# Differential attention inside a two-layer block: score products on 64 rows, alternating between the two maps

## The chip, the cores and the metric

The kernel runs on one core of a Trainium2 chip. A core has a matrix engine, TensorE (PE in the profile, with its weight loads shown as PEld), a vector engine (DVE), a scalar engine (ACT), a general engine (POOL), and a queue (SP) that here issues all transfers between the chip's memory and the on-chip memory, and within the latter. Products are accumulated in a small memory of their own, PSUM. The metric is the time of one launch in microseconds, as the median of several runs.

## What is computed

The reference is two layers of a block over 512 latent tokens x and 256 context tokens ctx, with width 1024. Layer 0 mixes tokens with differential attention, layer 1 with a short gated convolution; each is followed by a SwiGLU feed-forward part, with RMSNorm and adaLN modulation ahead of every part. The change lies in the attention of layer 0, cut here to what matters:

```python
def diff_attention(h, hc, wqkv, lam, subln_g, wo, cos, sin, layer_idx, need_ctx):
    ...
    scale = HEAD_DIM ** -0.5                      # HEAD_DIM = 64, DA_HEADS = 8
    def project(t):
        q, k, v = jnp.split(t @ wqkv, 3, axis=-1)
        return (q.reshape(B, n, DA_HEADS, 2, HEAD_DIM),
                k.reshape(B, n, DA_HEADS, 2, HEAD_DIM),
                v.reshape(B, n, DA_HEADS, DA_VDIM))
    def attend(qb, kk, vv):
        s = jnp.einsum('bqhmd,bkhmd->bhmqk', qb, kk).astype(jnp.float32) * scale
        p = jax.nn.softmax(s, axis=-1)
        p = p[:, :, 0] - lam_full * p[:, :, 1]
        return jnp.einsum('bhqk,bkhe->bqhe', p.astype(vv.dtype), vv)
    ...
```

Each head has two score maps (m = 0 and 1), each from 64 of the head's 128 query and key components. The softmax of the second map, times a learned factor, is taken from that of the first, and the difference is applied to the values. The 512 latent queries look at 768 keys, latent and context.

## The kernel before

Activations are held transposed, with features on the 128 partitions and tokens along the free dimension. All large products are made from a high and a low part of each float32 operand: `split` (lines 53 to 55) rounds the source to the high part on ACT and has DVE subtract it for the low part. `mm3` (line 77) then issues three products, high by high, high by low and low by high.

`finish_q` and `finish_k` take the projected queries and keys of a head out of PSUM, apply the rotation (`rope`, on ACT, DVE and POOL) and split them into `qt` and `kt`. Partitions 0 to 63 belong to map 0, 64 to 127 to map 1. `halves_to` (line 432) then moves them with eight transfers a head, all on the SP queue (line 438): for each map it puts the 64 rows of the queries twice on top of each other, for high and low (`qs`), and the keys' high part above their low part (`ks`). With 128 rows filled that way, one product adds two of the four partial products at once: query-high and query-low each meet the stack of key-high and key-low, so that four products of the parts come from two instructions.

`attend` (line 508) goes over the four query blocks of a head, 32 blocks of 128 queries in all. For each block and map it makes scores S of 128 x 768 in a PSUM tile (line 528): two key ranges (512 and 256 columns) by two products. The tag "S" has two buffers, so the tile of one map is free again when the exponential of the same place in the block before is done. Then come a row maximum on DVE (line 532), the exponential on ACT (line 536), the combination of the two maps on DVE (line 546), six transposes on PE (line 551), and for every second block the product with the values (`po`). Between the blocks stand generators that make the projections of later heads (`psq`, `psk`, `pskc`, `psv`), the adaLN rows (`ada`, `araw`) and, at the end, the output projection (`poa`, `pob`).

The order on each engine is not written out by hand: a scheduler with a timeline of its own places every instruction once its operands are due, so score products and projections are interleaved on PE. Within `attend` nothing is fixed before the change.

Of the kernel before, what the change touches and what calls it, by code (L numbers as in the profile page):

```python
# [11 lines left out]
F32 = mybir.dt.float32  # L12
F32R = mybir.dt.float32r
# [5 lines left out]
P = 128  # L19
# [5 lines left out]
def block_kernel(  # L25
# [11 lines left out]
    nc = tc.nc  # L37
    T = x.shape[1]
# [4 lines left out]
    KV = T + C  # L43
# [9 lines left out]
    def split(hi, lo, src):  # L53
        nc.scalar.copy(hi, src)  # L54
        nc.vector.tensor_tensor(lo, src, hi.bitcast(F32), op=ALU.subtract)  # L55
# [55 lines left out]
    psB = tc.alloc_tile_pool(name="psB", bufs=2, space=PSUM)  # L111
# [8 lines left out]

    for tag, n, bufs in (
        [(f"Or{h}", 512, 1) for h in range(NH)] + [("qs0", 1024, 2), ("qs1", 1024, 2)]
        + [("e", 768, 3), ("pth", 768, 3), ("ptl", 768, 3), ("ks0", 768, 2), ("ks1", 768, 2)]
        + [(f"v{p}{t}", 256, 2) for t in range(KB) for p in "hl"]
        + [("sq", 512, 1), ("dg0", 512, 1), ("dg1", 512, 1)]
        + [(t, 4, 2) for t in ("sv", "sr", "rh", "rl")] + [(t, 4, 3) for t in ("rr", "mx")] + [("ss", 8, 2), ("den", 8, 2)]
        + [("ld", 2, 1)]
        + [("araw", 1024, 2), ("ada", 1024, 1), ("qt", 1024, 1), ("kt", 1536, 1), ("rcos", 512, 1), ("rsin", 512, 1)]
        + [("sw", 512, 1), ("rt", 512, 2)]
    ):  # L130
        ap.tile([P, n], F32, tag=tag, bufs=bufs, name=f"place_{tag}")
# [4 lines left out]
    xt_dram = nc.dram_tensor("xt_spill", [DB, P, T], F32, kind="Internal").ap()  # L136

    rows = lambda v: v.rearrange("(j p) -> j p", p=P)
    st1, st2 = (ap.tile([P, P], F32, tag=t, name=n) for t, n in (("ks1", "st1"), ("ks1", "st2")))
    nc.vector.memset(st1, 0.0)  # L140
    nc.vector.memset(st2, 0.0)
    nc.sync.dma_start(st1[0:8, :], rows(c[0]))
# [26 lines left out]
    cn = [nat(ctx, t, "qs1", 2, f"cn{t}") for t in range(CB)]  # L169
# [37 lines left out]
    def nat_rstd(src, tag, name):  # L207

        nb = len(src)
        ss = ap.tile([P, 8], F32, tag="ss", name=f"ss{name}")  # L210
        for t in range(nb):
            for f in range(2):
                junk = ap.tile([P, 512], F32, tag="sq", bufs=1, name=f"junk{name}")
                nc.scalar.activation(
                    junk, src[t][:, f * 512:(f + 1) * 512], AF.Square,
                    accum_out=ss[:, t + 4 * f:t + 4 * f + 1],
                )
        v = ap.tile([P, 4], F32, tag="sv", name=f"sv{name}")[:, :nb]
        nc.vector.tensor_tensor(v, ss[:, :nb], ss[:, 4:4 + nb], op=ALU.add)
        nc.vector.tensor_scalar(v, v, 1.0 / D, EPS, op0=ALU.mult, op1=ALU.add)  # L220
        r = ap.tile([P, 4], F32, tag="sr", name=f"sr{name}")[:, :nb]
        nc.gpsimd.tensor_tensor(r, v, mhalf[:, :nb], op=ALU.pow)
        ps = spread(r, nb, "pt", name)
        o = ap.tile([P, 512], F32, tag=tag, bufs=2 if tag == "ks0" else 1, name=f"rs{name}")[:, :nb * P]
        nc.vector.tensor_copy(o, ps)
        return o

# [37 lines left out]

    XT0 = [ap.tile([P, T], F32, tag=f"Or{k}", bufs=1, name=f"XT{k}") for k in range(DB)]
    rx = nat_rstd(xn, "sw", "x")
    for k in range(0, DB, 2):
        pt = psB.tile([P, 2, T], F32, tag="S", name=f"ptx{k}")
        for a in range(2):  # L270
# [2 lines left out]
            nc.vector.tensor_copy(XT0[k + a], pt[:, a, :])  # L273
        if k == 0:
            ada0(0, raws0)
    rc = nat_rstd(cn, "ks0", "c")
    ctt = [ap.tile([P, 4, C], F32, tag="araw", name=f"ct{i}") for i in range(2)]
    CT = [ctt[k // 4][:, k % 4, :] for k in range(DB)]
    for i in range(2):
        pt = psB.tile([P, 4, C], F32, tag="S", name=f"ptc{i}")  # L280
        for a in range(4):
# [3 lines left out]
        for a in (0, 2):  # L285
            nc.scalar.copy(ctt[i][:, a:a + 2, :], pt[:, a:a + 2, :])
    vps = [psB.tile([P, 1024], F32, tag="S", name=f"vps{i}") for i in range(2)]
    qps = psB.tile([P, 512], F32, tag="acc", name="qps")
# [140 lines left out]
        eng.tensor_tensor(r, r, s, op=ALU.add)  # L429
        return r  # L430

    def halves_to(dst, src, both):

        for m in range(2):
            s = src[64 * m:64 * m + 64]
            for d in range(2):
                o = dst[m][64 * d:64 * d + 64]
                nc.sync.dma_start(
                    o.bitcast(F32), (s if both else s[:, d, :]).bitcast(F32)
                )  # L440

    def finish_q(h, ps):

        r = rope(ps, HD ** -0.5, f"q{h}")
        qt = ap.tile([P, 2, T], F32R, tag="qt", bufs=1, name=f"qt{h}")
        split(qt[:, 0, :], qt[:, 1, :], r)
        q = [ap.tile([P, 2, T], F32R, tag=f"qs{m}", name=f"qs{h}_{m}") for m in range(2)]
        halves_to(q, qt, True)
        return q

    def finish_k(h, ps, psc):

        r = rope(ps, None, f"k{h}")
        kt = ap.tile([P, 2, KV], F32R, tag="kt", bufs=1, name=f"kt{h}")
        split(kt[:, 0, T:], kt[:, 1, T:], psc)
        split(kt[:, 0, :T], kt[:, 1, :T], r)
        ks = [ap.tile([P, KV], F32R, tag=f"ks{m}", name=f"ks{h}_{m}") for m in range(2)]
        halves_to(ks, kt, False)
        return ks

    def finish_v(g, t, ps):
# [46 lines left out]
    def attend(h, between, after=None):  # L508
        q, ks, vs = Q[h], K[h], V[h // 2]
        vc = slice((h % 2) * P, (h % 2) * P + P)  # L510
        O = ap.tile([P, T], F32, tag=f"Or{h}", bufs=1, name=f"O{h}")
        den = ap.tile([P, 2, TB], F32, tag="den", name=f"den{h}")
        for pr in range(2):
            pts = []
            for kh in range(2):
                pts.append(
                    (ap.tile([P, 3, 256], F32R, tag="pth", bufs=3, name=f"pth{h}_{pr}_{kh}"),
                     ap.tile([P, 3, 256], F32R, tag="ptl", bufs=3, name=f"ptl{h}_{pr}_{kh}"))
                )
            for s in range(2):  # L520
                qb = 2 * pr + s
                e = []
                mx = ap.tile([P, 2], F32, tag="mx", bufs=3, name=f"mx{h}_{qb}")
                for m in range(2):
                    S = psB.tile([P, 1024], F32, tag="S", name=f"S{h}_{qb}_{m}")
                    for a, b in ((0, 512), (512, KV)):
                        for j in range(2):
                            nc.tensor.matmul(  # L528
                                S[:, a:b], q[m][:, j, qb * P:(qb + 1) * P], ks[m][:, a:b],
                                start=(j == 0), stop=(j == 1),  # L530
                            )
                    nc.vector.tensor_reduce(  # L532
                        out=mx[:, m:m + 1], in_=S[:, :KV], axis=AX.X, op=ALU.max, negate=True
                    )
                    em = ap.tile([P, KV], F32, tag="e", bufs=3, name=f"e{h}_{qb}_{m}")
                    nc.scalar.activation(  # L536
                        em, S[:, :KV], AF.Exp, bias=mx[:, m:m + 1], accum_out=den[:, m, qb:qb + 1]
                    )
                    e.append(em)

                rr = ap.tile([P, 1], F32, tag="rr", bufs=3, name=f"rr{h}_{qb}")
                nc.vector.reciprocal(rr, den[:, 1, qb:qb + 1])
                nc.vector.scalar_tensor_tensor(
                    rr, rr, nlam, den[:, 0, qb:qb + 1], op0=ALU.mult, op1=ALU.mult
                )
                nc.vector.scalar_tensor_tensor(e[0], e[1], rr, e[0], op0=ALU.mult, op1=ALU.add)
                for kh in range(2):
                    pt = psB.tile([P, 512], F32, tag="pt", name=f"pt{h}_{qb}_{kh}")[:, :3 * P]
                    for i in range(3):
                        k = 3 * kh + i  # L550
                        nc.tensor.transpose(pt[:, i * P:(i + 1) * P], e[0][:, k * P:(k + 1) * P], ident)
                    cs = slice(s * P, (s + 1) * P)
                    split(pts[kh][0][:, :, cs], pts[kh][1][:, :, cs], pt.rearrange("p (k c) -> p k c", c=P))
                between()
            po = psB.tile([P, 512], F32, tag="pt", name=f"po{h}_{pr}")[:, :256]
            for k in range(KB):
                ph, pl = pts[k // 3]
                mm3(po, vs[k][0][:, vc], vs[k][1][:, vc], ph[:, k % 3, :], pl[:, k % 3, :], k == 0, k == KB - 1)
            nc.scalar.copy(O[:, pr * 256:(pr + 1) * 256], po)
            if after:  # L560
                On[h] = O
                after(pr, den)
        On[h] = O
        if not after:
            later.append(subnorm(h, den, 0, TB))
# [395 lines left out]
```

## Time and profile before

| what | value |
|---|---|
| median of 3 runs | 1371.27 us (1370.04 to 1371.96) |
| the profiled execution, its own time | 1369.84 us |
| its span, first to last instruction | 1368.1 us |
| PE busy | 1312.1 us, 7052 products |
| DVE busy | 780.4 us |
| ACT busy | 529.6 us |
| POOL busy | 244.8 us |
| DMA, 16 engines | 44.7% of their time, 181.65 MB |

How to read it: the span is what the profile sees of the profiled execution, and the remaining 1.7 us lie around it. Products on PE are pipelined: a product's duration reaches from its start to its result, and the next one starts long before that, so the cost of one product in a stream is the distance between two starts. The heads run from about 108 us (first score product) to about 401 us (last).

### The profile page before, as it was taken

The page shows a single profiled execution, that of the slowest core. Times are in us where ns is not written, and L with a number is a line of the kernel's source. Part 1 is how long each engine was busy: PE and PEld are TensorE (multiplying, and loading weights), DVE is VectorE, ACT ScalarE, POOL GpSimd, SP SyncE. Part 2 cuts the span into 40 slices and gives each one's busy share as a digit, 9 for nine tenths or more (in the row PEclk, how much of TensorE's full clock was granted, in tenths as well). Part 3 has the DMA queues.
Part 4 walks back from the last instruction along what each step waited for, and adds up shares of the span by engine and source line. Part 5 has one row for each costly group of instructions (what it writes and reads, how often), then busy time and mean ns, then how long its engine had stood idle before and what let it go on. Part 6 is the DMA issues. An engine that isn't in the chain of part 4 may idle for free.

```text
span 1368.1 us, 18008 instructions
## 1 busy us (share of the span) xinstructions
PE 1312.1 (96%) x7052; PEld 1128.1 (82%) x7052; DVE 780.4 (57%) x1043; ACT 529.6 (39%) x872; POOL 244.8 (18%) x197
## 2 busy tenths in 40 slices
PE   6889899899999999999999999999999999999997
PEld 4678799798888988888888889888988888888887
DVE  6886976777886766776753255444473333332322
ACT  6655646454555432333222244222362232232222
POOL 3244635524314100000001041000340000000000
PEclk9999999999999999999999999999999999999999
DMA  8957633623432666666643333333333333333321
GB/s 291 271 151 219 189 101 124 152 80 93 135 97 80 197 206 200 219 222 203 212 128 96 100 93 93 93 98 88 92 93 99 102 92 93 106 91 109 94 78 62
DMA packets 238742, 182.79 MB, mean 134 GB/s; under 512 B 6937, under 2 KB 220226, under 8 KB 238658
## 3 DMA queue, kind: packets, MB, share of 16 engines
q1 hardware_dynamic: 238658, 181.65, 44.7%
q8 instruction: 55, 0.90, 0.3%
q14 instruction: 29, 0.24, 0.1%
HBM read 162.75 MB, written 4.19 MB: 122 GB/s over the span
## 4 chain that ended last, share of the span: by engine, by line
PE 79%; DVE 8%; DMA 4%; ACT 4%; issue 2%; POOL 2%; SPq 0%; DVEq 0%; ACTq 0%; POOLq 0%
PE po_fo L78 6%; PE po_fo L79 6%; PE po_fo L80 6%; PE pb L79 5%; PE pb L78 5%; PE pb L80 5%; PE pa L78 5%; PE pa L79 5%; PE pa L80 5%; DMA araw<-in_ada_w_dram 3%; PE S L528 2%; PE psc L79 1%; PE psb L80 1%; PE psu L80 1%; PE psc L80 1%
## 5 line engine op out<-in xcount | busy, mean ns | idle before, releaser
L54 ACT CAST whi_f<-raw_f 128x1024 fp32r<-128x1024 f32 x87 | 91.4, 1051 | 234.6 <-issue 117.9
L55 DVE TENSOR_TENSOR wlo_f<-raw_f,whi_f 128x1024 fp32r<-128x1024 f32 x87 | 107.4, 1234 | 79.2 <-ACT whi_f L54 76.2
L55 DVE TENSOR_TENSOR wlo_fo<-raw_fo,whi_fo 128x1024 fp32r<-128x1024 f32 (+1 forms) x48 | 54.5, 1135 | 118.4 <-ACT whi_fo L54 116.8
L607 POOL TENSOR_TENSOR nacc<-nacc,nsq 128x256 f32<-128x256 f32 x30 | 30.7, 1023 | 494.1 <-ACT nsq L603 493.6
L78 PE MATMUL po_fo<-uh,whi_fo 128*128 128x512 f32 (+1 forms) x324 | 118.8, 367 | 0.1
L79 PE MATMUL po_fo<-ul,whi_fo 128*128 128x512 f32 (+1 forms) x324 | 118.7, 366 | 0.0
L80 PE MATMUL po_fo<-uh,wlo_fo 128*128 128x512 f32 (+1 forms) x324 | 118.6, 366 | 0.0
L54 ACT CAST whi_fo<-raw_fo 128x1024 fp32r<-128x1024 f32 (+1 forms) x48 | 47.1, 981 | 177.6 <-PE po_fo L79 146.9
L378 DVE SCALAR_TENSOR_TENSOR ada<-araw,sil,ada 128x1024 f32<-128x1024 f32 x49 | 62.9, 1284 | 39.0 <-DMA araw<-in_ada_w_dram 38.7
L803 DVE TENSOR_TENSOR uu<-sl,pb 128x512 f32<-128x512 f32 (+1 forms) x48 | 30.7, 640 | 81.5 <-PE pb L80 77.2
L536 ACT ACTIVATE e<-S,mx 128x768 f32<-128x768 f32 x64 | 57.8, 904 | 46.7 <-DVE mx L532 36.1
L80 PE MATMUL pb<-h2h,wlo_f 128*128 128x512 f32 (+1 forms) x192 | 71.8, 374 | 0.0
L78 PE MATMUL pa<-h3h,whi_f 128*128 128x512 f32 (+1 forms) x192 | 71.6, 374 | 0.0
L79 PE MATMUL pb<-h2l,whi_f 128*128 128x512 f32 (+1 forms) x192 | 71.5, 372 | 0.0
L78 PE MATMUL pb<-h2h,whi_f 128*128 128x512 f32 (+1 forms) x192 | 71.4, 372 | 0.0
L78 PE MATMUL pb<-h3h,whi_f 128*128 128x512 f32 (+1 forms) x192 | 71.4, 372 | 0.0
L79 PE MATMUL pb<-h3l,whi_f 128*128 128x512 f32 (+1 forms) x192 | 71.4, 372 | 0.0
L80 PE MATMUL pa<-h3h,wlo_f 128*128 128x512 f32 (+1 forms) x192 | 71.4, 372 | 0.0
L80 PE MATMUL pb<-h3h,wlo_f 128*128 128x512 f32 (+1 forms) x192 | 71.4, 372 | 0.0
L79 PE MATMUL pa<-h3l,whi_f 128*128 128x512 f32 (+1 forms) x192 | 71.2, 372 | 0.0
L78 PEld LDWEIGHTS po_fo<-uh,whi_fo 128*128 128x128 f32 x324 | 61.2, 189 | 10.1 <-DVE on L890 0.3
L79 PEld LDWEIGHTS po_fo<-ul,whi_fo 128*128 128x128 f32 x324 | 61.1, 189 | 9.9
(362 smaller groups left out, 3715.2 us busy)
## 6 DMA issues: line engine op xcount, KB each, us to landing
raw_f<-in_ffn_w_in_dram SPq DMA_DIRECT2D x88, 512.0 KB, 3.6
araw<-in_ada_w_dram SPq DMA_DIRECT2D x80, 512.0 KB, 4.4
raw_fo<-in_ffn_w_out_dram SPq DMA_DIRECT2D x32, 512.0 KB, 3.7
raw_a<-in_ada_w_dram SPq DMA_DIRECT2D x32, 256.0 KB, 4.6
qs<-qt SPq DMA_DIRECT2D x32, 256.0 KB, 4.9
raw_wv<-in_da_wqkv_dram SPq DMA_DIRECT2D x12, 512.0 KB, 5.0
ks<-kt SPq DMA_DIRECT2D x32, 192.0 KB, 4.8
raw_fo<-in_ffn_w_out_dram SPq DMA_DIRECT2D x16, 384.0 KB, 4.0
```

Of the source, the lines that this page charges most:

```text
L54: nc.scalar.copy(hi, src)
L55: nc.vector.tensor_tensor(lo, src, hi.bitcast(F32), op=ALU.subtract)
L78: nc.tensor.matmul(ps, sh, mh, start=start, stop=False)
L79: nc.tensor.matmul(ps, sh, ml, start=False, stop=False)
L80: nc.tensor.matmul(ps, sl, mh, start=False, stop=stop)
L378: nc.vector.scalar_tensor_tensor(acc, raw, s, acc, op0=ALU.mult, op1=ALU.add)
L528: nc.tensor.matmul(S[:, a:b], q[m][:, j, qb * P:(qb + 1) * P], ks[m][:, a:b], start=(j == 0), stop=(j == 1),)
L536: nc.scalar.activation(em, S[:, :KV], AF.Exp, bias=mx[:, m:m + 1], accum_out=den[:, m, qb:qb + 1])
L607: nc.gpsimd.tensor_tensor(acc, acc, sq, op=ALU.add)
L803: nc.vector.tensor_tensor(u, s, pb, op=ALU.mult)
```

## The change

The queries and keys of a head are no longer moved. `split` writes the high and low parts to one tile each (`q`, and `ks` under the new tag "kk"), with map 0 on partitions 0 to 63 and map 1 on 64 to 127, as they come. A score product now uses the 64 rows of its map alone. High by high, high by low and low by high are three products for each map and key range, so 12 for a block instead of 8, and low by low is left out. Both S tiles are taken ahead, the products of the two maps alternate, and a region in which the scheduler keeps PE's written order (`manual_schedule`) holds the 12 products in that order among themselves; other products may still be placed between them. `halves_to` and its 64 transfers are gone. Tags and one small buffer are moved accordingly.

```diff
-        + [("e", 768, 3), ("pth", 768, 3), ("ptl", 768, 3), ("ks0", 768, 2), ("ks1", 768, 2)]
+        + [("e", 768, 3), ("pth", 768, 3), ("ptl", 768, 3), ("kk", 1536, 2)]
...
-    def halves_to(dst, src, both):
-
-        for m in range(2):
-            s = src[64 * m:64 * m + 64]
-            for d in range(2):
-                o = dst[m][64 * d:64 * d + 64]
-                nc.sync.dma_start(
-                    o.bitcast(F32), (s if both else s[:, d, :]).bitcast(F32)
-                )
-
     def finish_q(h, ps):
 
         r = rope(ps, HD ** -0.5, f"q{h}")
-        qt = ap.tile([P, 2, T], F32R, tag="qt", bufs=1, name=f"qt{h}")
-        split(qt[:, 0, :], qt[:, 1, :], r)
-        q = [ap.tile([P, 2, T], F32R, tag=f"qs{m}", name=f"qs{h}_{m}") for m in range(2)]
-        halves_to(q, qt, True)
+        q = ap.tile([P, 2, T], F32R, tag="qs0", bufs=2, name=f"q{h}")
+        split(q[:, 0, :], q[:, 1, :], r)
         return q
 
     def finish_k(h, ps, psc):
 
         r = rope(ps, None, f"k{h}")
-        kt = ap.tile([P, 2, KV], F32R, tag="kt", bufs=1, name=f"kt{h}")
-        split(kt[:, 0, T:], kt[:, 1, T:], psc)
-        split(kt[:, 0, :T], kt[:, 1, :T], r)
-        ks = [ap.tile([P, KV], F32R, tag=f"ks{m}", name=f"ks{h}_{m}") for m in range(2)]
-        halves_to(ks, kt, False)
+        ks = ap.tile([P, 2, KV], F32R, tag="kk", bufs=2, name=f"ks{h}")
+        split(ks[:, 0, T:], ks[:, 1, T:], psc)
+        split(ks[:, 0, :T], ks[:, 1, :T], r)
         return ks
...
-                for m in range(2):
-                    S = psB.tile([P, 1024], F32, tag="S", name=f"S{h}_{qb}_{m}")
+
+                Ss = [psB.tile([P, 1024], F32, tag="S", name=f"S{h}_{qb}_{m}") for m in range(2)]
+                with tc.manual_schedule(engines={mybir.EngineType.PE}):
                     for a, b in ((0, 512), (512, KV)):
-                        for j in range(2):
-                            nc.tensor.matmul(
-                                S[:, a:b], q[m][:, j, qb * P:(qb + 1) * P], ks[m][:, a:b],
-                                start=(j == 0), stop=(j == 1),
-                            )
+                        for j, (jq, jk) in enumerate(((0, 0), (0, 1), (1, 0))):
+                            for m in range(2):
+                                r = slice(64 * m, 64 * m + 64)
+                                nc.tensor.matmul(
+                                    Ss[m][:, a:b], q[r, jq, qb * P:(qb + 1) * P], ks[r, jk, a:b],
+                                    start=(j == 0), stop=(j == 2),
+                                )
+                for m, S in enumerate(Ss):
                     nc.vector.tensor_reduce(
```

PE, head 1, block 1, before. `S_1_0` and `S_1_1` are the score tiles of map 0 and map 1 (the first number is the block, the second the map), `pskc` the context keys of the next head, `pt` the transposes of the block before:

```order
L528 MATMUL S_1_0_1591<-ks_0_1401,qs_0_1333 128x512 x2
L528 MATMUL S_1_0_1591<-ks_0_1401,qs_0_1333 128x256 x2
L78 MATMUL pskc_1845<-ch_154,whi_wk_1775 128x256
L79 MATMUL pskc_1845<-cl_155,whi_wk_1775 128x256
L80 MATMUL pskc_1845<-ch_154,wlo_wk_1776 128x256
```

The four products of map 0 stand together, those of map 1 follow later in the same way, after other products.

PE, the same block after the change, where `po` is the product with the values of the head before and `psv` a value projection:

```order
L80 MATMUL po_1_1281<-pth_1_1_1191,vl_5_1050 128x256
L517 MATMUL S_1_0_1601<-ks_1405,q_1345 128x512
L80 MATMUL psv_4_1919<-whi_wv_0_1909,cl_154 128x256
L78 MATMUL psv_4_1919<-whi_wv_0_1909,ch_155 128x256
L517 MATMUL S_1_1_1602<-ks_1405,q_1345 128x512
L517 MATMUL S_1_0_1601<-ks_1405,q_1345 128x512
L517 MATMUL S_1_1_1602<-ks_1405,q_1345 128x512
L517 MATMUL S_1_0_1601<-ks_1405,q_1345 128x512
L517 MATMUL S_1_1_1602<-ks_1405,q_1345 128x512
L517 MATMUL S_1_0_1601<-ks_1405,q_1345 128x256
L517 MATMUL S_1_1_1602<-ks_1405,q_1345 128x256
```

The first product of map 0 stands alone between products on 128 rows, the other eleven alternate behind the first product of map 1. Of the 32 blocks 26 have such a lone first product, and all score products together form 74 stretches.

SP, before, from the last load of the first adaLN row on. `qs` and `ks` are the moved queries and keys, `raw_wv` is a weight and `araw` a row block of the adaLN matrix:

```order
L366 DMA araw_2_7_1733<-in_ada_w_dram 128x1024
L438 DMA qs_0_1064<-qt_1061 64x1024 x2
L438 DMA qs_1_1065<-qt_1061 64x1024 x2
L438 DMA ks_0_1082<-kt_1077 64x768 x2
L438 DMA ks_1_1083<-kt_1077 64x768 x2
L69 DMA raw_wv_0_1888<-in_da_wqkv_dram 128x4x256
L366 DMA araw_3_0_1998<-in_ada_w_dram 128x1024
```

SP, the same place after the change:

```order
L366 DMA araw_2_7_1764<-in_ada_w_dram 128x1024
L69 DMA raw_wv_0_1907<-in_da_wqkv_dram 128x4x256
L366 DMA araw_3_0_2024<-in_ada_w_dram 128x1024
L366 DMA araw_3_1_2046<-in_ada_w_dram 128x1024
L69 DMA raw_wv_1_1913<-in_da_wqkv_dram 128x4x256
```

The loads that stood behind the eight transfers follow one another directly.

## Rows read from the trace of the kernel before

**Rows 1.** The page: busy time by engine, and the chain by engine.

```profile
PE 1312.1 (96%) x7052; PEld 1128.1 (82%) x7052; DVE 780.4 (57%) x1043; ACT 529.6 (39%) x872; POOL 244.8 (18%) x197
...
PE 79%; DVE 8%; DMA 4%; ACT 4%; issue 2%; POOL 2%; SPq 0%; DVEq 0%; ACTq 0%; POOLq 0%
```

**Rows 2.** Stretches: length, busy PE, PEld, DVE, ACT, POOL; clock, DMA, GB/s.

```profile
100.00:150.00 50.00, 45.30 (x303) 40.71 (x301) 36.14 (x52) 28.95 (x52) 28.06 (x15) 1.00 0.70 201
150.00:200.00 50.00, 44.95 (x282) 40.27 (x281) 42.37 (x62) 26.79 (x50) 23.89 (x15) 0.93 0.56 154
200.00:250.00 50.00, 44.23 (x304) 40.73 (x304) 36.70 (x57) 30.16 (x55) 29.96 (x18) 0.97 0.42 121
250.00:300.00 50.00, 50.00 (x345) 46.89 (x344) 37.05 (x65) 25.00 (x50) 17.49 (x14) 0.96 0.45 116
300.00:350.00 50.00, 48.26 (x296) 43.38 (x297) 36.17 (x63) 24.51 (x52) 18.47 (x14) 0.97 0.32 81
350.00:400.00 50.00, 47.06 (x262) 40.83 (x262) 42.90 (x70) 24.01 (x48) 12.78 (x11) 0.97 0.47 131
...
500.00:550.00 50.00, 50.00 (x221) 41.36 (x221) 33.95 (x36) 15.20 (x19) 0.00 (x0) 1.00 0.71 220
```

**Rows 3.** Waits of PE, 100 to 450 us: total us, times, longest.

```profile
PE psv L78 <- DVE kt L55: 5.7, 1, 5.7
PE S L528 <- ACT e L536: 5.4, 3, 3.7
...
PE S L528 <- DMA ks<-kt: 2.8, 1, 2.8
```

**Rows 4.** Groups by shape: busy us, mean ns of one; idle before, releasers.

```profile
L528 PE MATMUL S<-ks,qs 128*128 128x512 f32 x128 | 43.6, 416 | 8.2 <-ACT e L536 5.4 <-DMA ks<-kt 2.8
```

**Rows 5.** Timeline of PE, 200 to 225 us: start, duration, instruction.

```profile
205.59 0.28 PE L78 MATMUL psv<-whi_wv,hh 128*128 128x256 f32 x1
205.71 0.28 PE L79 MATMUL psv<-wlo_wv,hh 128*128 128x256 f32 x1
...
210.90 0.87 PE L528 MATMUL S<-ks,qs 128*128 128x512 f32 x4
211.60 0.73 PE L385 MATMUL pada<-ones_f,ada 128*128 128x1 f32 x6
212.19 0.48 PE L204 MATMUL spro<-dg0o,ones_r 128*128 128x512 f32 x1
...
217.17 0.40 PE L80 MATMUL psq<-hh,wlo_wq 128*128 128x512 f32 x1
217.40 0.40 PE L78 MATMUL psq<-hh,whi_wq 128*128 128x512 f32 x1
```

**Rows 6.** Timeline of PE around the transposes of four rows.

```profile
32.50 0.28 PE L79 MATMUL vps<-w0l,ch 128*128 128x256 f32 x1
32.71 0.28 PE L256 MATMUL pmt<-ident,mr 4*128 4x4 f32 x2
32.92 0.28 PE L248 MATMUL pm<-whi_a,cst 128*4 128x256 f32 x1
```

**Rows 7.** Transfers of head 0 on SP, then waits of SP and ACT.

```profile
98.98 3.16 SPq L438 DMA_DIRECT2D qs<-qt  x4
102.23 3.66 SPq L438 DMA_DIRECT2D ks<-kt  x4
105.94 0.61 SPq L69 DMA_DIRECT2D raw_wv<-in_da_wqkv_dram  x1
...
SPq L438 <- DVE qt L55: 35.2, 7, 8.9
...
ACT araw L373 <- DMA araw<-in_ada_w_dram: 10.6, 9, 2.1
```

More of the change, by code (lines that the diff above doesn't have):

```diff
@@ L138, in block_kernel @@
     rows = lambda v: v.rearrange("(j p) -> j p", p=P)
-    st1, st2 = (ap.tile([P, P], F32, tag=t, name=n) for t, n in (("ks1", "st1"), ("ks1", "st2")))
+    st1, st2 = (ap.tile([P, P], F32, tag=t, name=n) for t, n in (("kk", "st1"), ("kk", "st2")))
     nc.vector.memset(st1, 0.0)
@@ L223, in nat_rstd @@
         ps = spread(r, nb, "pt", name)
-        o = ap.tile([P, 512], F32, tag=tag, bufs=2 if tag == "ks0" else 1, name=f"rs{name}")[:, :nb * P]
+        o = ap.tile([P, 512], F32, tag=tag, bufs=1, name=f"rs{name}")[:, :nb * P]
         nc.vector.tensor_copy(o, ps)
@@ L275, in block_kernel @@
             ada0(0, raws0)
-    rc = nat_rstd(cn, "ks0", "c")
+    rc = nat_rstd(cn, "kt", "c")
     ctt = [ap.tile([P, 4, C], F32, tag="araw", name=f"ct{i}") for i in range(2)]
```

## The prediction

> **What bounds the kernel now.** I read the page first [rows 1]: TensorE (PE) is busy in 96% of the span, and 79% of the chain that ended last is PE work. A busy PE is not PE at its peak, so the second view is the table by stretches [rows 2]. From 500 us on PE is busy in 50.00 of 50 us, with one product starting as soon as the array lets it; there nothing but the number and the spacing of products sets the time. From 100 to 400 us, where the eight attention heads run, PE is busy in 45.30, 44.95, 44.23, 50.00, 48.26 and 47.06 us of each 50: 279.8 of 300, so 20.2 us without work. Where the change acts is therefore a stage that PE bounds for the most part, with holes that other engines make. The third view names the holes [rows 3]: the largest are 5.7 us, once, for a VectorE (DVE) pass over kt; 5.4 us in three waits of score products for an exponential that has to free their PSUM tile; 2.8 us, once, for the transfer of keys of head 0. The last two belong to the lines that the change touches.
>
> The compiled order tells where a shift can arise. PE's rows of the two programs are the same up to the first score product of head 0, and the same again in the last 4626 rows, which begin soon after the last score products. All that differs runs from about 99 us [rows 7] to a little over 400. What comes after is PE without holes (the last row of [rows 2]), so a microsecond won or lost there reaches the end whole.
>
> **The score products themselves.** Spacing, not duration, is the price of a product in a stream. Products of 512 columns start 0.23 us apart (217.17, 217.40), of 256 columns 0.12 us apart (205.59, 205.71) [rows 5]. A map's scores are now four products, two of each width: 2 x 0.23 + 2 x 0.12 = 0.70 us, and the timeline has just that (210.90 to 211.60) [rows 5]. There are 32 blocks of two maps, which agrees with the 128 products of 512 columns of the grouped view [rows 4]: 64 x 0.70 = 44.8 us of PE.
>
> After the change a map has six products, three of each width, on 64 rows. If the products of the two maps, which lie on different halves of the rows, run together, a block takes 3 x 0.23 + 3 x 0.12 = 1.05 us. The order takes part of this back: in 26 of the 32 blocks the first product of map 0 stands alone, with other work behind it, because the first product of map 1 waits for a PSUM tile of its own. It finds no partner, and map 1 still has its six: 0.23 + 1.05 = 1.28 us. Together 26 x 1.28 + 6 x 1.05 = 39.6 us, the low bound. The high bound with overlap comes from the weights: each product loads 128 columns, and the products of one column, which consist of little but their load, start 0.59 / 6 = 0.098 us apart (211.60 to 212.19) [rows 5]. If the loads of the two halves follow each other, a pair of 256 columns takes 0.20 us and not 0.12: 32 x 3 x 0.08 = 7.7 us more, 47.3. I take 42, nearer the low end: a product of 256 columns starts 0.12 us after the one before it although each brings a load of about 0.098, so loads run under products, and only the narrow pairs can feel a second one. Against 44.8 that is **-2.8 us** (-5.2 to +2.5).
>
> **The edges.** PE now changes between products on 128 rows and on 64. I count 74 separate stretches of score products in the new order, each with an edge into and out of it. No 64-row product exists in the trace; the nearest row is the small transpose of four rows, L256 [rows 6]. The product of 256 columns ahead of it starts at 32.50, the transpose at 32.71: 0.21 instead of 0.12, so 0.09 us for the way in. The two transposes take 0.21 us until the next product starts, where two products of one column take 2 x 0.098 = 0.20: 0.01 us for the way out. Behind a wide product the way out may cost as much as the way in, so I take 0.05, half way. 74 x 0.14 = **+10.4 us**; the bounds are nothing (the 64-row form behaves better than this row) and a full drain at both edges, below. The Trainium skill speaks against the change here: "TensorEngine Tiling (Array Packing)", section Key Properties, says that changing the tiling mode drains TensorE. Hanging on that rule: the 0.09 us of L256 is about half of what a full drain would lay bare, so the trace bears it out in part; by the rule in full the sum is that of the second rival.
>
> **What goes away.** 64 transfers leave the SP queue, eight for each head. For head 0 SP issues them from 98.98 to about 105.9, 3.16 and 3.66 us [rows 7], and PE's 2.8 us wait for the last of them [rows 3] goes. Later heads find their keys long there, so nothing more is won on PE directly. SP also stands still before them, 35.2 us in seven waits for DVE's qt [rows 7], with loads of weights and of the adaLN matrix queued behind; ScalarE (ACT) waits 10.6 us for that matrix in nine waits [rows 7], with exponentials behind it. That can shorten the 5.4 us of score waits [rows 3], the most that this is worth: 2.8 to 8.2 us in all. I take **-4 us**, near the low end, because DVE and ACT keep the same instructions (1025 and 773 rows in either order) and DVE is busy in 42.37 of the 50 us from 150 on [rows 2]. What is late next there is DVE.
>
> **The new wait.** The 12 products of a block are now tied into one order, so map 0's scores cannot finish before the PSUM tile of map 1 is free, which needs the second exponential of the block before; everything on PE stands behind that product. The order puts other products ahead of it in 26 blocks. I cost it at nothing, covered by these; uncovered it is the fourth rival. The split into high and low parts writes the same elements to another tile, and the dropped fourth product (low times low) is already in the count of six: no cost.
>
> **The sum.** -2.8 + 10.4 - 4.0 = +3.6 us. The profiled execution took 1369.84 us with a span of 1368.1; the median of the runs is 1371.27, so 1.4 us above. On the median the sum gives 1374.9, rounded to **1375**; from the bounds of its terms but the drain the case spans 1369 to 1382.
>
> **The rivals.** (1) *The edges cost nothing*, the next load slipping under the running product as it does within a stream [rows 5]: -2.8 - 4, or with the best of each term -5.2 - 8.2: 1358 to 1365, say 1364.5. For it speaks that entering the one-column products costs nothing visible (210.90 to 211.60 is the plain 0.70) [rows 5], against it L256. (2) *Each edge drains the array.* A product of 256 columns lasts 0.28 us and its successor starts after 0.12 [rows 5]: 0.16 us that a drain would lay bare, 148 times, 23.7 us. -2.8 + 23.7 - 4 = +16.9: 1388. This is the slower side: with the other terms as they stand the time is over 1374 from 0.064 us an edge on. It is the rule of the Trainium skill cited above, in full. (3) *The halves don't run together*, so the alternation doesn't do what it is written for: 192 products of each width one after the other, 192 x 0.35 = 67.2 us, +22.4; +22.4 + 10.4 - 4 = +28.8: 1400. Nothing in the trace shows two products at once, and nothing in the operands, other rows and other PSUM tiles, ties them. The Trainium skill, "TensorE: Matmul & The Clock Gate", section Measured speedup vs the span model, has products in different row groups start about 4 ns apart; no run here shows it, and by it this rival would not arise. (4) *The tied order makes PE wait.* The three waits that are there average 1.8 us [rows 3]; if half of the 26 blocks had one, cut to 1.2 us by the work put ahead, it would be 15.6 us on top of the sum: 1390.5.
>
> **How the numbers follow.** Forecast 0.41; rival 1 0.31; rival 2 0.13; rival 3 0.09; rival 4 0.06. About 0.2%, 2.7 us, is what a measurement of this kernel can tell from no change, that is 1368.5 to 1374. Of the forecast's own range about half lies above that, 0.20, and 0.17 within it, 0.04 below. Rival 1 is nearly all faster, 0.29, with 0.02 within. The others are slower, 0.28. Together: faster 0.33, same 0.19, slower 0.48. The range 1361 to 1390 leaves out the third rival and the far ends of the first and the fourth, 0.2 in all. Both signs have weight; the likeliest case alone is 1369 to 1382.
>
> **What would show it.** In the new profile: the start of map 1's product beside map 0's (a few ns apart if they run together, 0.23 us if not); a paired block of about 1.05 to 1.2 us; the spacing into and out of a stretch, 0.21 against 0.12 for a 256-column neighbour if the edges cost 0.09; no wait for ks; the two waits on exponentials longer or gone; the stretches from 500 us on unchanged. I am wrong if the edges are free, if the halves take turns, or if PE's idle time between 100 and 400 us moves by more than the 4 us.

## The result, and the profile after

The change makes the kernel slower: 1383.31 us, median of 4 runs (1380.93 to 1388.73), against 1371.36 for the kernel before beside it. The ratio is 1.0091, with a 95% interval of 1.0073 to 1.0109. A second measurement of both gave 1384.78 against 1371.08: 1.0108 (1.0091 to 1.0125). The profiled execution took 1380.93 us with a span of 1379.2, 11.1 longer than before.

The page of the changed kernel, busy time and chain by engine:

```profile
PE 1331.8 (97%) x7180; PEld 1123.5 (81%) x7180; DVE 782.0 (57%) x1043; ACT 529.0 (38%) x872; POOL 241.2 (17%) x197
...
PE 79%; DVE 7%; DMA 5%; ACT 3%; POOL 3%; issue 2%; SPq 0%; ACTq 0%; DVEq 0%; POOLq 0%
```

Against [rows 1], PE has 128 products more and is busy 19.7 us longer. The other engines do what they did. So the time went to PE, and the next view says where. Each of the two rows below covers the same work, from the first key projection of head 1 to the first product of the feed-forward part; first the kernel before, then the changed one (columns as in [rows 2]):

```profile
93.10:437.30 344.20, 320.01 (x2050) 288.69 (x2048) 265.72 (x421) 182.97 (x352) 151.44 (x108) 0.97 0.46 128
```

```profile
91.90:447.80 355.90, 340.01 (x2176) 285.50 (x2176) 267.47 (x421) 182.40 (x352) 148.07 (x108) 0.98 0.27 82
```

The stage grew by 11.7 us, which is the whole difference of the spans (the start came 1.2 earlier, what follows takes 0.6 longer). Inside it PE is busy 20.0 us more, and its idle time fell from 24.2 to 15.9, by 8.3. Behind the stage PE is full, as before [rows 2]:

```profile
500.00:550.00 50.00, 50.00 (x222) 41.25 (x221) 33.31 (x36) 15.39 (x19) 0.00 (x0) 1.00 0.68 215
```

The 20 us stand in the timeline of PE. Here is a lone first product of a block in the changed kernel, between products on 128 rows (start, duration, instruction):

```profile
227.81 0.28 PE L80 MATMUL po<-pth,vl 128*128 128x256 f32 x1
227.93 0.28 PE L78 MATMUL po<-pth,vh 128*128 128x256 f32 x1
228.13 0.49 PE L517 MATMUL S<-ks,q 64*128 64x512 f32 x1
228.56 0.50 PE L80 MATMUL psk<-hh,wlo_wk 128*128 128x512 f32 x1
228.89 0.40 PE L78 MATMUL psk<-hh,whi_wk 128*128 128x512 f32 x1
229.13 0.39 PE L79 MATMUL psk<-hl,whi_wk 128*128 128x512 f32 x1
```

Undisturbed, a product of 256 columns is followed after 0.12 us and one of 512 after 0.23 [rows 5]. Here the steps are 0.20, 0.43, 0.33 and 0.24 (starts are rounded to 0.01). The way into 64 rows makes the first start late by 0.08. The step behind it is late by 0.20, and the one after that by 0.10. In a longer stretch that 0.20 comes apart: in blocks of six pairs the second pair starts 0.11 late, and the first product behind the block 0.09 late. So **every switch between 128 and 64 rows makes two starts late, by about 0.09 and 0.11 us**, and a stretch, with two switches, costs 0.39 us (medians in the changed kernel: 0.09, 0.11, 0.09, 0.10; in a stretch of one product the second and the third fall on one step). The weight loads (PEld) at the same place show what is late:

```profile
227.81 0.19 PEld L78 LDWEIGHTS po<-pth,vh 128*128 128x128 f32 x1
228.13 0.18 PEld L517 LDWEIGHTS S<-ks,q 64*128 64x128 f32 x1
228.55 0.19 PEld L80 LDWEIGHTS psk<-hh,wlo_wk 128*128 128x128 f32 x1 [0.24 <-issue]
228.66 0.19 PEld L78 LDWEIGHTS psk<-hh,whi_wk 128*128 128x128 f32 x1
228.90 0.19 PEld L79 LDWEIGHTS psk<-hl,whi_wk 128*128 128x128 f32 x1
```

In the stream a product's load starts with the product before it (227.81 for the product at 227.93, 228.90 for that at 229.13), so it runs ahead. The first load behind each of the two switches (228.13, 228.55) starts only with its own product, and the next one (228.66) starts 0.10 us behind the product before it. Both late starts go with late loads. A wait for data is not the cause: the product that the last experiment puts in reads operands that have long been there, and switches cost the same around it. The waits that leave PE idle have shrunk; PE, 100 to 460 us of the changed kernel (total us, times, longest):

```profile
PE psv L78 <- DVE ks L55: 3.4, 2, 2.6
...
PE S L517 <- ACT e L526: 1.6, 2, 1.0
```

In [rows 3] the score products waited 5.4 us for exponentials and 2.8 for the transfer of keys. Now 1.6 are left of the first and the second is gone.

### The profile page after: what moved, and what is told of

Read it like the earlier page. It is cut to its first block, busy times and chain, and to the rows that moved or that the text cites. A ratio compares the mean times of both kernels' runs of the same rounds, so it can differ in the third digit from the quotient of the medians.

```text
span 1379.2 us, 18102 instructions
## 1 busy us (share of the span) xinstructions
PE 1331.8 (97%) x7180; PEld 1123.5 (81%) x7180; DVE 782.0 (57%) x1043; ACT 529.0 (38%) x872; POOL 241.2 (17%) x197
## 4 chain that ended last, share of the span: by engine, by line
PE 79%; DVE 7%; DMA 5%; ACT 3%; POOL 3%; issue 2%; SPq 0%; ACTq 0%; DVEq 0%; POOLq 0%
PE po_fo L78 6%; PE po_fo L79 6%; PE po_fo L80 6%; PE pa L78 5%; PE pa L79 5%; PE pa L80 5%; PE pb L79 5%; PE pb L80 5%; PE pb L78 5%; DMA araw<-in_ada_w_dram 3%; PE S L517 2%; POOL ada L374 1%; PE pt L541 1%; PE psc L79 1%; PE psb L79 1%
## 5 line engine op out<-in xcount | busy, mean ns | idle before, releaser
L522 DVE TENSOR_REDUCE mx<-S 128x1 f32<-128x768 f32 x64 | 58.2, 948 | 20.4 <-PE S L517 20.3
L80 PEld LDWEIGHTS po_fo<-uh,wlo_fo 128*128 128x128 f32 x324 | 61.1, 189 | 9.9
```

The lines of the kernel that those rows point to most:

```text
L80: nc.tensor.matmul(ps, sl, mh, start=False, stop=stop)
L522: nc.vector.tensor_reduce(out=mx[:, m:m + 1], in_=S[:, :KV], axis=AX.X, op=ALU.max, negate=True)
```

## The experiments

**One stretch for a block.** Theory 1 was that the 74 stretches cost their edges, theory 2 that the tied order makes PE wait for the second PSUM tile. In the first version a block's first product also waits for the second exponential of the block before, and the region has priority in the scheduler, so that nothing comes between its products: 33 stretches, 31 of them whole blocks.

```diff
+    prev_exp = []
...
-                with tc.manual_schedule(engines={mybir.EngineType.PE}):
+                with tc.high_priority(), tc.manual_schedule(engines={mybir.EngineType.PE}):
...
-                                nc.tensor.matmul(
+                                mmi = nc.tensor.matmul(
...
+                                if prev_exp and a == j == m == 0:
+                                    tc.add_manual_dep(mmi.ins, prev_exp[-1].ins.name, ...)
...
-                    nc.scalar.activation(
+                    ex = nc.scalar.activation(
...
+                prev_exp.append(ex)
```

> The changed kernel, with the 12 score products of a block held together: the first product also waits for the second exponential of the block before, and the region has a high priority for the scheduler. The order then has 33 stretches of score products instead of 74 and hardly a lone first product. Theory 1 (PE pays for edges): the trace after shows about 0.39 us for every stretch (0.09 in, 0.20 out, 0.10 on the next product), and a lone product costs another 0.22. 41 x 0.39 + 26 x 0.22 = 22 us less than the change, about 1361 to 1365, faster than the kernel before. Theory 2 (the time comes from waiting for the second PSUM tile): the first product now waits longer than before, so no gain or a loss, 1383 or above.

Measured: 1368.13 us against 1370.71 before, ratio 0.9982 (0.9970 to 0.9993): 3 us above theory 1's range, and far below theory 2's. The second version has the added wait alone, without the priority, and 51 stretches.

> Only the added wait of the first product, without the high priority: 51 stretches in the order, few lone products. Theory 1: 23 x 0.39 + about 22 x 0.22 = 14 us less than the change, about 1369. Theory 2: 1383 or above.

Measured: 1367.24, ratio 0.9977 (0.9966 to 0.9989). The same stage in the two, in that order:

```profile
94.90:435.30 340.40, 319.81 (x2177) 279.55 (x2176) 262.98 (x421) 182.34 (x352) 145.02 (x108) 0.97 0.28 86
```

```profile
94.20:435.10 340.90, 324.85 (x2177) 281.35 (x2176) 265.85 (x421) 183.16 (x352) 151.12 (x108) 0.97 0.28 86
```

With the same 384 score products on 64 rows PE is busy 20.2 and 15.2 us less than in the change. Theory 2 falls: both versions wait at least as strictly for the second tile (their score products wait 4.2 and 4.0 us for exponentials, against 1.6 in the change), and are 15 to 18 us faster. A whole block in the first version, between transposes:

```profile
215.46 1.32 PE L519 MATMUL S<-ks,q 64*128 64x512 f32 x12
216.71 0.55 PE L550 MATMUL pt<-ident,e 128*128 128x128 f32 x3
217.01 0.48 PE L78 MATMUL psq<-hh,whi_wq 128*128 128x512 f32 x1
```

From the first start to the next instruction 1.25 us: the 1.05 of six pairs, and the 0.20 of the two late starts in it. The two halves do run together: in this block the records of each pair start 3 to 4 ns apart.

**The maps in turn.** The same version, but map 0's six products and then map 1's six, to price the running together.

```diff
-                    for a, b in ((0, 512), (512, KV)):
-                        for j, (jq, jk) in enumerate(((0, 0), (0, 1), (1, 0))):
-                            for m in range(2):
+                    for m in range(2):
+                        for a, b in ((0, 512), (512, KV)):
+                            for j, (jq, jk) in enumerate(((0, 0), (0, 1), (1, 0))):
```

> As the kernel with one stretch for each block, but the six products of map 0 first and then the six of map 1: 33 stretches, so the same edges, and no two halves at once. If the alternation makes the halves run together, this costs 3 x 0.23 + 3 x 0.12 = 1.05 us more in each of 32 blocks, 33 us over the kernel with one stretch (about 1395), less what other engines' holes absorb. If the halves run one after the other in both, the two times agree within 3 us.

Measured: 1375.51, ratio 1.0042 (1.0028 to 1.0055): between the two. The stage, and a block:

```profile
95.00:442.60 347.60, 336.09 (x2176) 296.84 (x2175) 259.84 (x421) 182.99 (x352) 149.39 (x108) 0.98 0.28 84
```

```profile
212.98 1.90 PE L519 MATMUL S<-ks,q 64*128 64x512 f32 x12
214.81 0.55 PE L550 MATMUL pt<-ident,e 128*128 128x128 f32 x3
```

A block takes 1.83 us instead of 1.25, not the 2.1 and more of twelve products in turn, since the records show a partial overlap: map 1's first product starts 6 to 7 ns behind map 0's third, ahead of three narrow products of map 0 that stand before it in the program. And of the 16.3 us by which PE is busier than in the first version, only 7.4 reach the time.

**The transfers put back.** To price their going, the change with the 64 transfers on SP as before, into tiles that nobody reads (`halves_to` comes back as it was):

```diff
         split(q[:, 0, :], q[:, 1, :], r)
+        halves_to(
+            [ap.tile([P, 2, T], F32R, tag="qs1", name=f"dq{h}_0"),
+             ap.tile([P, 2, T], F32R, tag="qt", bufs=1, name=f"dq{h}_1")], q, True)
...
+        dk = ap.tile([P, 2, KV], F32R, tag="kt", bufs=1, name=f"dk{h}")
+        halves_to([dk[:, m, :] for m in range(2)], ks, False)
```

> The changed kernel with the 64 transfers of queries and keys put back, of the same sizes and on the same queue, into tiles that nobody reads. The order of PE has 74 stretches as the change has. PE's extra work by the trace after is over 20 us, the time moved by 12: about 10 us were won elsewhere. Theory A (the transfers themselves cost that, by the SP queue and the loads behind it): 1390 or above. Theory B (it was won because the scores no longer wait for a transfer, so heads start earlier): within 3 us of the change, 1380 to 1386.

Measured: 1376.80, ratio 1.0055 (1.0041 to 1.0069). Neither expectation: it is faster than the change. A transfer that nobody reads can't gain time by itself, so the change was timed again in a second measurement, where the same transfers were also put into the version with one stretch (the first diff and this one together).

> The change unaltered, timed beside the kernel before once more, since its first runs spread from 1381 to 1389 us and the version with the transfers put back came out at 1377. Theory 1 (74 edges in and out of 64-row work at about 0.39 us, 29 us of PE): 1379 to 1385. Rival (the transfers that were put back do not cost but help, or the first job was a slow one): equal to the version with the transfers, 1375 to 1378.

> The version with one stretch per block, and the 64 transfers put back on SP into tiles that nobody reads. Theory 1 (the transfers cost SP's time alone): equal to that version, 1366 to 1370. Rival (their going is worth the 4 us of the prediction's sum): 1371 to 1374; by the upper bound of that term, 8.2, up to 1376.

Measured: the change 1384.78 (given above), the version with one stretch and transfers 1367.59 against 1371.08, ratio 0.9971 (0.9960 to 0.9983). Without them the ratio was 0.9982 (0.9970 to 0.9993). In this order the transfers cost nothing that can be measured. In the change's own order the version without them is 6.5 to 8 us slower. Most of that lies at one place, where the output projection (`poa`) first needs the heads' outputs. Two stretches of 5 us there, of the change and then of the version with its transfers put back (length, busy PE, PEld, DVE, ACT, POOL; clock, DMA, GB/s):

```profile
360.00:365.00 5.00, 1.81 (x8) 0.76 (x6) 5.00 (x6) 5.00 (x12) 4.61 (x4) 0.90 0.56 190
365.00:370.00 5.00, 4.78 (x11) 3.80 (x12) 4.96 (x11) 1.46 (x4) 0.00 (x0) 0.50 0.18 51
```

```profile
360.00:365.00 5.00, 4.48 (x19) 2.83 (x19) 5.00 (x11) 4.81 (x11) 1.35 (x1) 1.00 0.90 254
365.00:370.00 5.00, 5.00 (x28) 3.87 (x27) 4.93 (x9) 0.59 (x1) 1.96 (x1) 1.00 0.37 124
```

The change has 3.4 us without work on PE, while DVE is full, and behind that the granted clock is 0.50, the 1.2 GHz level, for the next 5 us:

```profile
366.24 0.63 PE L78 MATMUL poa<-o,whi_woa 128*128 128x512 f32 x1
366.66 0.63 PE L79 MATMUL poa<-o,whi_woa 128*128 128x512 f32 x1
```

Products of 512 columns start 0.43 us apart there instead of 0.23; over the dozen of them that is 2.4 us. The hole and the slow dozen make 5.8 us against 0.5, and the stages of these two profiled runs differ by 4.9, 355.90 and this:

```profile
92.70:443.70 351.00, 336.63 (x2178) 283.47 (x2176) 264.22 (x421) 182.05 (x352) 149.72 (x108) 0.99 0.45 125
```

The kernel before has a hole at the same place, 2.9 us:

```profile
360.00:365.00 5.00, 2.06 (x10) 1.67 (x9) 4.99 (x10) 4.39 (x10) 4.29 (x4) 0.81 0.98 315
```

Why the scheduler's order avoids it in the one version is not settled. Both have 74 stretches, so what differs is the order around them and transfers that nobody reads, and that moves the time by as much as the forecast missed by.

**The kernel before, with its maps together.** Since one stretch won time, the same wait and priority were put around the eight products of a block in the kernel before, its 128 rows and transfers as they were.

```diff
-                for m in range(2):
-                    S = psB.tile([P, 1024], F32, tag="S", name=f"S{h}_{qb}_{m}")
-                    for a, b in ((0, 512), (512, KV)):
-                        for j in range(2):
+                Ss = [psB.tile([P, 1024], F32, tag="S", name=f"S{h}_{qb}_{m}") for m in range(2)]
+                with tc.high_priority(), tc.manual_schedule(engines={mybir.EngineType.PE}):
+                    for m in range(2):
+                        for a, b in ((0, 512), (512, KV)):
+                            for j in range(2):
...
```

> The kernel before, its 128-row products and its transfers unaltered, but with the eight products of a block's two maps kept in one stretch that starts when both PSUM tiles are free, as in the version with one stretch per block. On 128 rows a stretch has no edge to pay, so PE's own work stays at 64 x 0.70 = 44.8 us. Theory 1 (the 64-row form itself is worth 44.8 against 47, edges in, and the missing transfers little): within 3 us of the version with one stretch of 64-row products, 1364 to 1371; then what that version gains over the kernel before comes from the order and not from the 64 rows. Rival (the gain comes from the transfers that are gone): no better than the kernel before, 1370 to 1375.

Measured: 1363.79, ratio 0.9956 (0.9941 to 0.9971), the fastest of all kernels here. It is 3.8 us faster than the version with one stretch and transfers, a little more than theory 1's 3, and the rival's range is missed by 6. Its stage:

```profile
94.90:430.30 335.40, 317.69 (x2048) 286.71 (x2047) 267.75 (x421) 181.69 (x352) 152.23 (x108) 0.98 0.47 131
```

It is 8.8 us shorter than before, 2.3 by less busy PE and 6.5 by less idle time. Three of PE's waits, 100 to 450 us:

```profile
PE S L532 <- DMA ks<-kt: 3.2, 1, 3.2
...
PE psv L78 <- DVE kt L55: 1.2, 1, 1.2
...
PE S L532 <- ACT e L547: 0.3, 1, 0.3
```

The wait for the transferred keys is still there, but that for DVE's kt, 5.7 us in [rows 3], has shrunk to 1.2, and that of score products for exponentials, 5.4 us there, to 0.3. So the gain of the versions with one stretch over the kernel before came from the order, not from the 64 rows: with the maps together, 64 rows and the same transfers take 1367.59 and 128 rows 1363.79, measured together. Whether the wait or the priority makes it was not tried apart.

**The edge by itself.** The version with one stretch, and in the middle of each block one more product on 128 rows, of 256 columns, whose result nobody reads. It adds two switches a block and no other work than its own 0.12 us.

```diff
                     for a, b in ((0, 512), (512, KV)):
+                        if a:
+                            nc.tensor.matmul(
+                                Ss[0][:, KV:], q[:, 0, qb * P:(qb + 1) * P], ks[:, 0, :256],
+                                start=True, stop=True,
+                            )
```

> The version with one stretch per block, and in the middle of each block, between the wide and the narrow key range, one more product on 128 rows of 256 columns, whose result nobody reads. It costs 0.12 us of PE by itself and cuts the block in two, which adds one way in and one way out, 32 times. Theory 1 (0.39 us for a way in and out): a block takes 0.51 us more, 16.3 us of PE in all; the time rises by 6 to 16, 1374 to 1384. The prediction's price (0.14 us): 0.26 more a block, 8.3 us of PE, the time 1369 to 1376.

Measured: 1373.11, ratio 1.0021 (1.0009 to 1.0033). A block, and the stage:

```profile
220.16 0.96 PE L524 MATMUL S<-ks,q 64*128 64x512 f32 x6
221.05 0.38 PE L517 MATMUL S<-ks,q 128*128 128x256 f32 x1
221.36 0.63 PE L524 MATMUL S<-ks,q 64*128 64x256 f32 x6
221.92 0.66 PE L555 MATMUL pt<-ident,e 128*128 128x128 f32 x4
```

```profile
95.00:439.80 344.80, 332.60 (x2208) 281.19 (x2207) 265.25 (x421) 182.38 (x352) 150.09 (x108) 0.99 0.28 85
```

The three parts take 0.89, 0.31 and 0.56 us, where the plain spacings would be 0.69, 0.12 and 0.35: each is 0.19 to 0.21 late. The middle one lies between a way out and a way in, the other two between a way in and a way out. The block takes 1.76 instead of 1.25, 0.51 more, theory 1's 0.12 + 0.39. The prediction's 0.14 would have made it 0.26. The time rose by only about 5 us over the 1368 without the cut, a little below theory 1's range and inside that of the prediction's price. So the time alone would not have told the two apart; the block's length does. 12.8 us of busier PE became 4.4 us of stage: idle time fell from 20.6 to 12.2.

**One price list.** Six pairs for each of 32 blocks, 33.6 us; 0.39 for each stretch; 0.23 for each lone first product (another 0.12 for each product of the cut, and 0.58 a block for maps in turn). Beside it what the records give, from each score product's start to the next start, with holes over 0.35 us taken out and the lateness at the edges added:

| kernel | by the list, us | from the records, us | PE idle in the stage, us |
|---|---|---|---|
| before (64 x 0.70) | 44.8 | 48.8 | 24.2 |
| the change: 74 stretches, 26 lone | 33.6 + 28.9 + 6.0 = 68.5 | 69.2 | 15.9 |
| one stretch: 33 | 33.6 + 12.9 = 46.5 | 47.3 | 20.6 |
| added wait alone: 51 | 33.6 + 19.9 = 53.5 | 55.4 | 16.0 |
| maps in turn: 33 | 46.5 + 18.6 = 65.1 | 66.6 | 11.5 |
| cut in two: 67 | 33.6 + 26.1 + 3.8 = 63.5 | 64.3 | 12.2 |

PE's busy time differs between these kernels by up to 4.2 us otherwise than the records do: from one stretch to the cut 12.8 us, not 17.0. The granted clock of these two stages, 0.97 and 0.99, may be part of that; it was not priced apart.

## Why the prediction was right or wrong

The direction was right and the time lies in the range, but 1375 was 8 us short (10 by the second measurement), beyond the 1382 that the bounds of its terms, the drain left out, allowed, and two errors of opposite sign hide in it. That so little is left of them is luck: with the transfers put back, the same number of stretches took 1376.80. One of the signs that the prediction named for being wrong came true. PE's idle time from 100 to 400 us was to move by no more than 4 us; it fell from 20.2 to 11.4:

```profile
100.00:400.00 300.00, 288.56 (x1856) 240.84 (x1856) 223.39 (x345) 152.70 (x292) 124.29 (x82) 0.98 0.28 85
```

**The edges** are the term that was mis-sized: 10.4 us forecast, 28.9 measured (74 x 0.39). The step that failed is the reading of [rows 6]. Its 0.09 for the way in was right for the first start. The second late start was missing from the sum, on either side: it was never in those rows, where the two transposes start 0.08 apart and the wide products behind them 0.12 apart at once, as in a plain stream. And the way out was drawn from the same small transposes, 0.01, and set "half way" at 0.05. The 0.098 that it was measured against is a mean of unlike steps: single records show 0.03 behind the first one-column product and 0.11 behind the other five. Between products of 256 and 512 columns a way out costs what a way in does, 0.09 and then 0.10 to 0.11. The second rival, a drain at each of 148 edges for 0.16, named the mechanism that comes closest, with 23.7 us; its time, 1388, is the nearer one, and its price was still low: 0.16 for 0.195 an edge. The rule behind it, that a change of tiling mode drains TensorE (the Trainium skill, "TensorEngine Tiling (Array Packing)", section Key Properties), agrees with the cut blocks, where a switch loses about 0.20; the page gives no price. That the loads don't run ahead at a switch is shown above. Whether a drain holds them back, no run here tells: the load at 228.13 starts before the recorded end of the product before it (227.93 + 0.28), but these ends are modelled.

**The score products** were right, at the low bound: pairs start 3 to 4 ns apart and narrow pairs follow each other after 0.12, so the loads of two halves cost nothing visible; 33.6 and 6.0 for the lone products make the 39.6 forecast as low bound, where 42 was taken. Rival 3 falls with that. The Trainium skill's 4 ns ("TensorE: Matmul & The Clock Gate", section Measured speedup vs the span model) agrees with the measured 3 to 4. The kernel before had been taken 4 us too cheap, 44.8 for 48.8: a map's stretch of 0.70 takes 0.78 to 0.80 behind transposes, and a few ran at the lower clock. About 2 of these 4 us are only moved, though: 24 stretches start 0.03 behind a transpose, where transposes follow each other after 0.11. So PE's score work and its edges rose by 20 us by the records, 24 by the list, not by 7.6.

**The transfers** were not worth 4 us: with one stretch a block nothing, and in the change's own order the version without them is the slower one. The 2.8 us wait of head 0 did go [rows 3], and the first score product starts at 99.8 instead of 108.4; but the end of the stage does not follow the start of the first head: the fastest version here, with 128 rows and its maps together, has its first score product latest of all, at 110.6. That the 35.2 us of SP's standing still [rows 7] hold nobody up is shown by the version with one stretch, with and without transfers. What the 2.8 us wait alone was worth was not tried.

**The new wait** cost nothing, as forecast; rival 4 falls, with 1.6 us of such waits in the changed kernel.

**The second failed step** is in the sum, which takes every microsecond of PE work whole. The sentence behind it, that a microsecond won or lost reaches the end whole, holds for the length of the stage (11.7 us of it, 11.1 of the span), where PE has no holes behind it. It does not hold for work inside the heads' stage. There PE's holes wait for other engines, DVE above all, and work put on PE moves into them: of the 20.0 us, 8.3 went there. With the right prices (-5.2 + 28.9) and a full pass through, the time would have been 1395. The share that passes is not constant: 4.4 of 12.8 us in the cut version, 7.2 of 16.3 with the maps in turn, 6.8 of 16.6 for the change with transfers against before, and 11.7 of 20.0 for the change itself, the hole at `poa` included. Rival 1, free edges, is refuted by every stretch shown.

## What to carry to other kernels

A smaller row tile halves nothing if its products are scattered: count the stretches that the scheduler makes, price each at two switches (0.39 us here), and set that against what pairing saves (11.2 us here, 44.8 to 33.6), so that even one stretch a block, 12.9 us, gave no gain (1367.59 us against 1363.79 on 128 rows). Before rewriting the products, try the order by itself: keeping a block's products together won 0.44% with the old products. And in a stage where PE has holes, an added PE microsecond cost between a third and three fifths of one here, and another order of the same products, beside transfers that nobody reads, moved the time by 6.5 to 8 us. So test a price on the spacing of starts, not on the time.

## What the runs showed of the hardware

Between products of 256 and 512 columns a switch of row tiling delays two starts, not one, by 0.09 and 0.11 us, in both directions alike; the weight load behind the switch starts with its own product, where in a stream it starts with the product before. With the transposes of four rows [rows 6] the second delay was not to be seen. Products on different row halves need not start in program order: with the maps in turn, a product of map 1 started 6 to 7 ns behind map 0's third, ahead of three products that stand before it in the program, in 31 of 32 blocks. The Trainium skill ("TensorE: Matmul & The Clock Gate", section The mechanism) has products start strictly in program order; these records differ from it, where the two halves have no operand in common. Behind a hole of 3.4 us in which PE had only three long waits and a few products, the granted clock was 0.50 for about 5 us, and products of 512 columns started 0.43 us apart instead of 0.23.
